# A decoder layer's MLP in exact fp32 parts: six pairs of first-product tiles by Strassen's algorithm, on one core

## The chip, the core and the metric

The kernel runs on one core of one Trainium2 chip. The metric is device time in microseconds (us) of one execution, the median of three runs. In the rows of the profile, PE is the matrix engine TensorE (PEld its weight loads), DVE is VectorE, ACT is ScalarE, POOL is GpSimd, and SP issues most of the loads. SBUF is the on-chip memory, PSUM the banks into which matmuls add (one bank holds 128 × 512 fp32 values).

## The reference

One layer of a hybrid decoder with 512 tokens and 1024 channels. The part in front of the MLP (token mixing by pooling and a state-space branch, gates, and an output product) gives h and is the same before and after. The change lies in the MLP:

```python
v = rmsnorm(h, mlp_norm_w[i])
hid = jax.nn.relu(v @ w_ff1[i])      # (512 x 1024) @ (1024 x 4096)
h = h + (hid * hid) @ w_ff2[i]       # (512 x 4096) @ (4096 x 1024)
out = rmsnorm(h, final_norm_w)
```

## The kernel before, in words

**Numbers.** Every fp32 value of a product is held as two parts of type fp32r: a high part, which ScalarE makes by a cast, and a low part, which VectorE makes by subtracting the high part from the value. A product of 128 × 128 weights with 512 columns then takes three matmuls: high × high, high × low, low × high. For a block of weights (128 × 1024) `split()` (L840 the cast to `shi`, L841 the subtraction to `slo`) or `block_part` (L75 `whi`, L76 `wlo`) does this. The pairs of parts come from a pool of four buffers, and a cast waits until the last matmul that reads the pair four splits before has ended.

**Chunks.** The MLP goes in eight chunks (`NC = 8`) of 512 hidden columns. In the first product a chunk has four tiles of 128 hidden columns by 512 tokens. `ff1_tile` computes one with 24 matmuls of 512 columns into one PSUM bank `pf` (L99 to L101), then ScalarE takes Relu (L1045) and Square (L1046) into the chunk's tile `r`, of which there is one buffer. PSUM for these tiles comes from a pool of four banks; from chunk 0's S1 on, that product's sums hold two of them, and the tiles have the other two. With the fourth tile the chunk's hidden values are split: `hh` (L1058) and `hl` (L1059) for the values themselves, then four sums of token and column halves into a tile of their own, `s` (L1061 to L1064), and their high and low parts (L1065, L1066), which read `s` and no longer `r`.

**Second product.** For chunks 0 to 6 it is done by Strassen's algorithm: seven products of 12 matmuls of 512 columns, A11, S2, S3, A22, S4, A12 and S1. Each takes one of seven parts of hh and hl (`prod`, L1079 to L1081) and one split block: a quarter of the second matrix (`b11`, `b12`, `b22`, `b21`) or a sum of quarters. The four sums of a chunk are made by `sum_of` on GpSimd (L1090): t1 = b11 + b12 in place, t2 = t1 + b22, b12 + b22, and t2 + b21. A11, S2, S3 and A22 add into the same two PSUM banks `alpha`; after each, VectorE adds the partial result to the output tile `ht` (`onto`, L906, 128 × 1024), and the next product's first matmul waits for that add. S4 starts `alpha` anew. A12 and S1 add up in banks of their own over chunks 0 to 6.

**Order.** The program is written in the order in which work is meant to run: after A11, S2, S3 and A22 stands one `filler()`, one tile of a later chunk's first product. The blocks of weights are loaded by the SP queue in the order of `_weight_blocks`. A scheduler then places the instructions of each engine; within an engine they run strictly in that order, each waiting for its inputs and its buffer. Six tiles of the first product run ahead of chunk 0's A11.

Of the kernel before, what the change touches and what calls it, by code (L numbers as in the profile page):

```python
# [51 lines left out]
def kernel(ctx: ExitStack, tc, xT, x, w, vec, fnw, out):  # L52
# [56 lines left out]
    dve.tensor_copy(ones_r, ones_f)
# [726 lines left out]
    def split(src):  # L836
        hi = wp.tile([P, 1024], F32R, tag="whi", name=f"shi{nsplit[0]}")
        lo = wp.tile([P, 1024], F32R, tag="wlo", name=f"slo{nsplit[0]}")
        nsplit[0] += 1
        act.copy(hi, src)  # L840
        dve.tensor_tensor(lo, src, hi.bitcast(F32), op=ALU.subtract)  # L841
# [190 lines left out]
    def ff1_tile(c, f):  # L1034
        if pf:
            ps = pf.pop(0)[0]
        else:
            p = ff1_begin(c, f)
            ff1_part(p, range(NK), True, True)
            ps = p[0]  # L1040
        if f == 0:
# [3 lines left out]
        act.activation(r, ps, AF.Relu)  # L1045
        act.activation(r, r, AF.Square)  # L1046
# [11 lines left out]
        act.copy(hh[:, :, :3, :], r[:, :, :3, :])  # L1058
        dve.tensor_tensor(hl[:, :, :3, :], r[:, :, :3, :], hh[:, :, :3, :].bitcast(F32), op=ALU.subtract)  # L1059
# [2 lines left out]
        dve.tensor_tensor(s[:, :, 1, :], s[:, :, 0, :], r[:, :, 2, :], op=ALU.subtract)
        dve.tensor_tensor(s[:, :, 2, :], r[:, :, 0, :], s[:, :, 1, :], op=ALU.add)
# [1 line left out]
        act.copy(hh[:, :, 3:, :], s)  # L1065
        dve.tensor_tensor(hl[:, :, 3:, :], s, hh[:, :, 3:, :].bitcast(F32), op=ALU.subtract)  # L1066
# [263 lines left out]
```

## Time and profile before

| what | value |
|---|---|
| median of three runs | 1008.87 us (1008.87 to 1009.21) |
| the profiled execution's time | 1009.23 us |
| its span | 1007.4 us |
| TensorE busy | 999.4 us, 99% |
| VectorE busy | 713.7 us, 71% |
| ScalarE busy | 556.4 us, 55% |
| GpSimd busy | 88.7 us, 9% |
| start of the first chunk's A11 | 704.32 us in the span |
| end of the last matmul | 1001.52 us |

A row of a timeline has the start, the duration, the engine, the line of the program, the operation, output and inputs, the shape; in brackets stands the idle time of the engine before the instruction and what ended it. A row of a group has the count and then busy time and the mean of one in ns. A row of stretches has the stretch, its length, and for each engine busy time and count.

### The profile page before, as it was taken

What the parts mean: (1) busy time and instruction counts of PE and PEld (TensorE: products, weight loads), DVE (VectorE), ACT (ScalarE), POOL (GpSimd) and SP (SyncE); (2) the same over time, 40 slices, a digit from 0 to 9 for tenths busy, and PEclk for the clock granted to TensorE, in tenths of its full rate; (3) what the DMA queues carried; (4) which work ended last, traced back from release to release, by engine and by line L of the source; (5) the groups of instructions that cost most, each with busy time, mean ns of one, the idle gap of its engine ahead of it and who ended that gap; (6) DMA issues with size and microseconds to landing.
All of it is one profiled execution on the core that took longest, in us unless ns stands there. A gap on an engine that the chain in (4) does not pass through costs nothing.

```text
span 1007.4 us, 14025 instructions
## 1 busy us (share of the span) xinstructions
PE 999.4 (99%) x5689; PEld 871.7 (87%) x5689; DVE 713.7 (71%) x896; ACT 556.4 (55%) x785; POOL 88.7 (9%) x52
## 2 busy tenths in 40 slices
PE   9999999999999999999999999999999999999997
PEld 8889999898889999888898888888888888888886
DVE  8978777776745588686765557985766677666866
ACT  7756859595843659574244333565545445354444
POOL 0000000000000000000000001003040430412400
PEclk9999999999999999999999999999999999999999
DMA  7243232323233232324433235042333324323112
GB/s 241 68 140 112 64 126 84 118 75 129 81 123 88 81 107 86 131 80 145 167 102 105 88 101 186 2 168 84 106 97 111 109 81 126 104 84 126 42 42 85
DMA packets 29283, 105.64 MB, mean 105 GB/s; under 512 B 3297, under 2 KB 4257, under 8 KB 28193
## 3 DMA queue, kind: packets, MB, share of 16 engines
q1 hardware_dynamic: 26496, 92.75, 28.8%
q0 software_dynamic: 2000, 11.08, 3.0%
q8 instruction: 45, 0.74, 0.3%
q10 hardware_dynamic: 720, 0.91, 0.2%
q14 instruction: 22, 0.17, 0.1%
HBM read 102.55 MB, written 2.16 MB: 104 GB/s over the span
## 4 chain that ended last, share of the span: by engine, by line
PE 96%; DVE 2%; DMA 1%; ACT 0%; SPq 0%; issue 0%; ACTq 0%
PE px L157 6%; PE pf L100 6%; PE pf L99 6%; PE pf L101 6%; PE px L158 6%; PE px L160 6%; PE alpha L1079 3%; PE alpha L1080 3%; PE alpha L1081 3%; PE pz L160 3%; PE pz L157 3%; PE pz L158 3%; PE pp L160 2%; PE pp L157 2%; PE pp L158 2%; PE py L509 2%
## 5 line engine op out<-in xcount | busy, mean ns | idle before, releaser
L76 DVE TENSOR_TENSOR wlo<-raw,whi 128x1024 fp32r<-128x1024 f32 (+1 forms) x131 | 163.9, 1252 | 114.9 <-ACT whi L75 114.6
L75 ACT CAST whi<-raw 128x1024 fp32r<-128x1024 f32 (+1 forms) x131 | 136.0, 1041 | 126.3 <-PE pf L100 55.8
L157 PE MATMUL px<-uh,whi 128*128 128x264 f32 (+1 forms) x448 | 118.9, 286 | 0.0
L158 PE MATMUL px<-ul,whi 128*128 128x264 f32 (+1 forms) x448 | 117.5, 283 | 0.0
L99 PE MATMUL pf<-vh,whi 128*128 128x512 f32 x256 | 99.8, 390 | 0.0
L101 PE MATMUL pf<-vh,wlo 128*128 128x512 f32 x256 | 99.6, 389 | 0.0
L100 PE MATMUL pf<-vl,whi 128*128 128x512 f32 x256 | 99.6, 389 | 0.0
L160 PE MATMUL px<-uh,wlo 128*128 128x264 f32 (+1 forms) x448 | 90.3, 283 | 0.0
L157 PEld LDWEIGHTS px<-uh,whi 128*128 128x128 f32 x448 | 84.8, 189 | 1.3 <-issue 1.0
L158 PEld LDWEIGHTS px<-ul,whi 128*128 128x128 f32 x448 | 84.4, 188 | 0.0
L841 DVE TENSOR_TENSOR slo<-b,shi 128x1024 fp32r<-128x1024 f32 x35 | 49.1, 1403 | 31.6 <-ACT shi L840 31.6
L160 PEld LDWEIGHTS px<-uh,wlo 128*128 128x128 f32 x448 | 68.8, 188 | 0.0
L840 ACT CAST shi<-b 128x1024 fp32r<-128x1024 f32 x35 | 36.8, 1050 | 47.2 <-PE pf L100 36.4
L99 PEld LDWEIGHTS pf<-vh,whi 128*128 128x128 f32 x256 | 48.1, 188 | 10.0
L101 PEld LDWEIGHTS pf<-vh,wlo 128*128 128x128 f32 x256 | 48.0, 188 | 10.0
L1090 POOL TENSOR_TENSOR b<-b,b 128x1024 f32<-128x1024 f32 x14 | 35.6, 2544 | 238.3 <-DVE slo L841 238.3
L100 PEld LDWEIGHTS pf<-vl,whi 128*128 128x128 f32 x256 | 48.1, 188 | 9.9
L1079 PE MATMUL alpha<-shi,hh 128*128 128x512 f32 x140 | 54.6, 390 | 0.0
L1081 PE MATMUL alpha<-shi,hl 128*128 128x512 f32 x140 | 54.5, 389 | 0.0
L1080 PE MATMUL alpha<-slo,hh 128*128 128x512 f32 x140 | 54.5, 389 | 0.0
L906 DVE TENSOR_TENSOR ht<-ht,alpha 128x1024 f32<-128x1024 f32 x35 | 42.5, 1215 | 10.9 <-PE alpha L1081 10.9
L157 PE MATMUL pz<-uh,whi 128*128 128x512 f32 x112 | 43.7, 390 | 0.0
(419 smaller groups left out, 2471.1 us busy)
## 6 DMA issues: line engine op xcount, KB each, us to landing
raw<-in_w SPq DMA_DIRECT2D x129, 512.0 KB, 3.6
b<-in_w SPq DMA_DIRECT2D x28, 512.0 KB, 3.5
abc<-acs_d POOLq DMA_DIRECT2D x8, 1024.0 KB, 5.2
wob<-in_w SPq DMA_DIRECT2D x8, 512.0 KB, 5.9
xt<-in_xT SPq DMA_DIRECT2D x8, 264.0 KB, 5.8
ht<-in_x POOLq DMA_DIRECT2D x4, 512.0 KB, 7.1
w<-in_w SPq DMA_DIRECT2D x4, 512.0 KB, 3.4
out_dram<-out SPq DMA_DIRECT2D x4, 320.0 KB, 2.4
```

The costliest lines, as they stand in the source:

```text
L75: act.copy(hi[:, c], raw[:, c])
L76: dve.tensor_tensor(lo[:, c], raw[:, c], hi[:, c].bitcast(F32), op=ALU.subtract)
L99: pe.matmul(ps, ah, bh, start=first, stop=False)
L100: pe.matmul(ps, ah, bl, start=False, stop=False)
L101: pe.matmul(ps, al, bh, start=False, stop=last)
L157: pe.matmul(o, wh, rhs[0][k][:, c], start=k == 0, stop=False)
L158: pe.matmul(o, wh, rhs[1][k][:, c], start=False, stop=False)
L160: pe.matmul(o, wl, rhs[0][k][:, c], start=False, stop=k == NK - 1)
L841: dve.tensor_tensor(lo, src, hi.bitcast(F32), op=ALU.subtract)
L1079: pe.matmul(ps[t], a[0], wh[:, cs], start=f, stop=False, skip_group_check=True)
L1080: pe.matmul(ps[t], a[0], wl[:, cs], start=False, stop=False, skip_group_check=True)
L1081: pe.matmul(ps[t], a[1], wh[:, cs], start=False, stop=l, skip_group_check=True)
```

## The change

In chunks 2 to 7 the tiles 2 and 3 of the first product (`PAIRS`) are no longer two plain tiles of 24 matmuls of 512 columns, but one generator `strassen(c, p)` with seven products of 12 matmuls of 256 columns. Their right-hand sides are halves of v and four sums of its halves, which `sum_halves` makes and splits on VectorE and ScalarE for four pairs of channel blocks: two pairs (k = 0, 1) along the first six tiles, one each within chunk 0 (k = 2, 3). Their weights are two raw blocks and three sums of their halves, made on VectorE. The products use two PSUM banks, `fb[0]` and `fb[1]`; partial results are copied out to `c01` and `r` and added up there by ScalarE and VectorE. All first-product tiles now use these two banks, the first ones too, which had four before.

To make room, the sums of the hidden halves are made in place in `r` (`hid_of`), so the tile `s` is gone, and four small tiles moved; the final norm's weights are loaded in chunk 6 instead of at the start of the MLP. The order of S4, S1, S2 and S3 among the seven segments is another one. The first product is no longer filled in by whole tiles: `fill()` and `step()` take half a plain tile or one product of a pair at a time, as many as a chunk's `due` asks for, after each product of the second matrix. `QUARTERS_AT` gives the load order to match. The sums of the second matrix stay on GpSimd. In the program after, `split` has lines L845 and L846, `block_part` L78 and L79, `onto` L909.

```diff
+QUARTERS_AT = (7, 12, 16, 20, 24, 28, 32, 32)
...
-    fw = hp_.tile([P, D], F32, name="fw")
...
-    nc.gpsimd.dma_start(fw, fnw.partition_broadcast(P))
...
+    VS = {}
+    sums = []
+    work = [hid.tile([P, 2, 7, 256], F32, tag=t, name=f"work_{t}").rearrange("p a s t -> p (a s t)")
+            for t in ("hh", "hl")]
+    part_of = lambda i: work[i // 3][:, 1024 * (i % 3) : 1024 * (i % 3) + 1024]
+    for k in range(4):
+        hs = [m1p.tile([P, SEQ], F32R, tag=f"m1_{d}", name=f"sh{d}") for d in (k, k + 4)]
+        lo = slp.tile([P, 4, 256], F32R, tag=f"sl{k}", name=f"sl{k}")
+        f = part_of(4 + k % 2)
+        f1, f2 = f[:, :512], f[:, 512:]
+        t = part_of(k).rearrange("p (s t) -> p s t", s=4)
+        sums.append((hs, lo, t, f1, f2, k))
+        VS["A11", k], VS["A12", k] = (vh[k][:, T1], vl[k][:, T1]), (vh[k + 4][:, T1], vl[k + 4][:, T1])
+        VS["A22", k] = vh[k + 4][:, T2], vl[k + 4][:, T2]
+        for n, name in enumerate(("S1", "S2", "S4", "S3")):
+            VS[name, k] = hs[n // 2][:, 256 * (n % 2) : 256 * (n % 2) + 256], lo[:, n, :]
+
+    def sum_halves(k):
+        hs, lo, t, f1, f2, k = sums[k]
+        dve.tensor_tensor(f1, vh[k].bitcast(F32), vl[k].bitcast(F32), op=ADD)
+        dve.tensor_tensor(f2, vh[k + 4].bitcast(F32), vl[k + 4].bitcast(F32), op=ADD)
+        dve.tensor_tensor(t[:, 0, :], f1[:, T2], f2[:, T2], op=SUB)
+        dve.tensor_tensor(t[:, 1, :], t[:, 0, :], f1[:, T1], op=SUB)
+        dve.tensor_tensor(t[:, 2, :], f2[:, T1], t[:, 1, :], op=ADD)
+        dve.tensor_tensor(t[:, 3, :], f1[:, T1], f1[:, T2], op=SUB)
+        fl2 = lambda a, n: a[:, 2 * n : 2 * n + 2, :].rearrange("p s t -> p (s t)")
+        for n in range(2):
+            act.copy(hs[n], fl2(t, n))
+            dve.tensor_tensor(fl2(lo, n), fl2(t, n), hs[n].bitcast(F32), op=SUB)
...
+    PAIRS = {(c, 1) for c in range(2, NC)}
+    fb = [p[0] for p in pf]
...
+    def hid_of(c):
         r = rel[c]
         hh = hid.tile([P, 2, 7, 256], F32R, tag="hh", name=f"hh{c}")
         hl = hid.tile([P, 2, 7, 256], F32R, tag="hl", name=f"hl{c}")
+        rel[c] = (hh, hl)
+        m = 4 if c == NC - 1 else 3
+        act.copy(hh[:, :, :m, :], r[:, :, :m, :])
+        dve.tensor_tensor(hl[:, :, :m, :], r[:, :, :m, :], hh[:, :, :m, :].bitcast(F32), op=ALU.subtract)
         if c == NC - 1:
-            act.copy(hh[:, :, :4, :], r)
-            dve.tensor_tensor(hl[:, :, :4, :], r, hh[:, :, :4, :].bitcast(F32), op=ALU.subtract)
-            rel[c] = (hh, hl)
             return
-
-        act.copy(hh[:, :, :3, :], r[:, :, :3, :])
-        dve.tensor_tensor(hl[:, :, :3, :], r[:, :, :3, :], hh[:, :, :3, :].bitcast(F32), op=ALU.subtract)
-        s = tmp.tile([P, 2, 4, 256], F32, tag="sums", name=f"s{c}")
-        dve.tensor_tensor(s[:, :, 0, :], r[:, :, 3, :], r[:, :, 1, :], op=ALU.subtract)
-        dve.tensor_tensor(s[:, :, 1, :], s[:, :, 0, :], r[:, :, 2, :], op=ALU.subtract)
-        dve.tensor_tensor(s[:, :, 2, :], r[:, :, 0, :], s[:, :, 1, :], op=ALU.add)
-        dve.tensor_tensor(s[:, :, 3, :], r[:, :, 2, :], r[:, :, 3, :], op=ALU.subtract)
-        act.copy(hh[:, :, 3:, :], s)
-        dve.tensor_tensor(hl[:, :, 3:, :], s, hh[:, :, 3:, :].bitcast(F32), op=ALU.subtract)
-        rel[c] = (hh, hl)
+        dve.tensor_tensor(r[:, :, 1, :], r[:, :, 3, :], r[:, :, 1, :], op=ALU.subtract)
+        dve.tensor_tensor(r[:, :, 3, :], r[:, :, 2, :], r[:, :, 3, :], op=ALU.subtract)
+        dve.tensor_tensor(r[:, :, 2, :], r[:, :, 1, :], r[:, :, 2, :], op=ALU.subtract)
+        dve.tensor_tensor(r[:, :, 0, :], r[:, :, 0, :], r[:, :, 2, :], op=ALU.add)
+        act.copy(hh[:, :, 3:, :], r)
+        dve.tensor_tensor(hl[:, :, 3:, :], r, hh[:, :, 3:, :].bitcast(F32), op=ALU.subtract)
...
+    def strassen(c, p):
+        raw = []
+        for i in range(2):
+            b = nblk[0]
+            nblk[0] += 1
+            t = wp.tile([P, 1024], F32, tag="raw", name=f"raw{b}", bufs=3)
+            nc.sync.dma_start(t, w[b])
+            raw.append(t)
+        C1, C2 = slice(0, 512), slice(512, 1024)
+        t12 = wp.tile([P, 1024], F32, tag="raw", name=f"t12_{c}_{p}", bufs=3)
+        dve.tensor_tensor(t12[:, C2], raw[0][:, C1], raw[1][:, C1], op=ADD)
+        dve.tensor_tensor(t12[:, C1], t12[:, C2], raw[1][:, C2], op=ADD)
+        dve.tensor_tensor(raw[1][:, C1], raw[1][:, C1], raw[1][:, C2], op=ADD)
+        wA = split(raw[0])
+        yield 0
+        one, two = bank(), bank()
+        nth[0] += 1
+        al, be_, ga, de = one[:, T1], two[:, T2], two[:, T1], two[:, T2]
...
+        r = rel_of(c)[:, p]
+        product(al, "A11", wA, 0, True, False)
+        act.copy(c01[:, 0, :], al)
+        wB = split(t12)
+        yield 1
+        product(be_, "A12", wA, 512, True, True)
+        dve.tensor_tensor(c01[:, 0, :], c01[:, 0, :], be_, op=ADD)
+        dve.tensor_tensor(t12[:, C1], t12[:, C1], raw[0][:, C2], op=ADD)
+        yield 1
+        product(al, "S2", wB, 0, False, False)
+        act.copy(c01[:, 1, :], al)
+        wC = split(raw[1])
+        yield 1
+        product(ga, "S1", wB, 512, True, True)
+        dve.tensor_tensor(c01[:, 1, :], ga, c01[:, 1, :], op=SUB)
+        act.copy(r[:, 3, :], ga)
+        yield 1
+        product(al, "S3", wC, 0, False, False)
+        dve.tensor_tensor(r[:, 3, :], r[:, 3, :], al, op=SUB)
+        wD = split(t12[:, C1])
+        yield 1
+        product(de, "S4", wC, 512, True, True)
+        dve.tensor_tensor(c01[:, 1, :], c01[:, 1, :], de, op=ADD)
+        yield 1
+        product(al, "A22", wD, 0, False, True)
+        act.activation(r[:, 0:3:2, :], c01, AF.Relu)
+        act.activation(r[:, 1, :], al, AF.Relu)
+        act.activation(r[:, 3, :], r[:, 3, :], AF.Relu)
+        rf = r.rearrange("p s t -> p (s t)")
+        act.activation(rf, rf, AF.Square)
+        if p == 1:
+            hid_of(c)
+        yield 1
...
+    for n in range(6):
+        step()
+        step()
+        if n in (4, 5):
+            sum_halves(n - 4)
...
-    def filler():
-        if order:
-            ff1_tile(*order.pop(0))
+    due = [0, 0]
+
+    def fill(n=1):
+        due[0] += n * due[1]
+        while due[0] > 0.5 and (items or live):
+            due[0] -= step()

     for c in range(NC - 1):
+        assert nblk[0] - ff0 - 4 * c == QUARTERS_AT[c], (c, nblk[0] - ff0 - 4 * c)
         b11, b12, b22, b21 = (quarter(n) for n in ("b11_", "b12_", "b22_", "b21_"))
         z, e = c == 0, c == NC - 2
+        if c < NC - 3:
+            rest = sum(i[4] for i in items if i[1] < c + 2 or (i[1] == c + 2 and (i[2] == 0 if i[0] is strassen else i[2] < 2)))
+        else:
+            rest = sum(i[4] for i in items)
+        rest += sum(l[1] if l[1] > 2 else 2 * l[1] for l in live)
+        due[1] = rest / (7 if c < NC - 3 else 10 if c == NC - 3 else 3)
         prod(av, c, A11, split(b11), True, False)
         onto(0, 0, alpha, ADD)
         t1 = sum_of(b11, b12, "", b11)
         t2 = sum_of(t1, b22, f"t2_{c}")
-        filler()
+        fill()
         prod(av, c, S2, split(t2), False, False)
         onto(0, 1, alpha, SUB)
-        filler()
+        fill()
+        if z:
+            sum_halves(2)
         prod(av, c, S3, split(sum_of(b12, b22, "", b12)), False, False)
         onto(1, 1, alpha, SUB)
-        filler()
+        fill()
         prod(av, c, A22, split(sum_of(t2, b21, "", t2)), False, True)
         onto(1, 0, alpha, ADD)
+        if z:
+            sum_halves(3)
+        if e:
+            while items or live:
+                step()
+        else:
+            fill()
+        w22 = split(b22)
         if e:
             prod(q5v, c, S1, split(t1), z, True)
             for t in range(2):
                 onto(0, 1, q5v[t], ADD, t)
                 onto(1, 1, q5v[t], ADD, t)
-        elif c < NC - 3:
-            filler()
-        prod(av, c, S4, split(b22), True, True)
+            fw = slp.tile([P, D], F32, tag="sl1", name="fw")
+            nc.gpsimd.dma_start(fw, fnw.partition_broadcast(P))
+            junk2.append(m1p.tile([P, SEQ], F32, tag="m1_3", name="junk2"))
+        prod(av, c, S4, w22, True, True)
         onto(0, 1, alpha, ADD)
+        if not e:
+            fill()
         prod(p2v, c, A12, split(b21), z, False)
         if not e:
+            fill()
             prod(q5v, c, S1, split(t1), z, False)
-    assert not order
+            fill()
+    assert not items and not live
```

VectorE round A11 of chunk 0, before. `s` is the tile of hidden sums, `hl` the low parts of the hidden values, `slo` and `wlo` low parts of weights; L906 is the add of A11.

```order
L841 TENSOR_TENSOR slo_6673<-b_113_6664,shi_6672 128x1024
L76 TENSOR_TENSOR wlo_6694<-raw_6692,whi_6693 128x1024
L1061 TENSOR_TENSOR s_6582<-r_6507 128x2x256
L1064 TENSOR_TENSOR s_6582<-r_6507 128x2x256
L1062 TENSOR_TENSOR s_6582<-s_6582,r_6507 128x2x256
L1059 TENSOR_TENSOR hl_6579<-r_6507,hh_6578 128x2x768
L1063 TENSOR_TENSOR s_6582<-r_6507,s_6582 128x2x256
L841 TENSOR_TENSOR slo_6726<-t_0_6690,shi_6725 128x1024
L1066 TENSOR_TENSOR hl_6579<-s_6582,hh_6578 128x2x1024
L76 TENSOR_TENSOR wlo_6744<-raw_6742,whi_6743 128x1024
L906 TENSOR_TENSOR ht<-ht,alpha 128x2x512
```

VectorE at the same place, after. `r` is the hidden tile, now with the sums in it; L1048 to L1057 belong to `sum_halves`; L909 is the add of A11.

```order
L1052 TENSOR_TENSOR work_hh<-work_hl,work_hh 128x256
L1053 TENSOR_TENSOR work_hh<-work_hl 128x256
L1057 TENSOR_TENSOR sl_6513<-work_hh,sh_6511 128x512
L1048 TENSOR_TENSOR work_hl<-vh_6091,vl_6099 128x512
L1049 TENSOR_TENSOR work_hl<-vh_6095,vl_6103 128x512
L1096 TENSOR_TENSOR hl_6603<-r_6527,hh_6602 128x2x1024
L1057 TENSOR_TENSOR sl_6513<-work_hh,sh_6512 128x512
L1050 TENSOR_TENSOR work_hh<-work_hl 128x256
L1053 TENSOR_TENSOR work_hh<-work_hl 128x256
L1051 TENSOR_TENSOR work_hh<-work_hh,work_hl 128x256
L909 TENSOR_TENSOR ht<-ht,alpha 128x2x512
L1052 TENSOR_TENSOR work_hh<-work_hl,work_hh 128x256
```

The sums of v's halves stand between the hidden tile's sums (L1091 to L1094) and their low parts (L1096), and again between those and the add of A11. The split for S2 (`slo<-t`) now stands behind that add.

ScalarE at this place, before: `r` of chunk 1 is written (L1045) after the cast of chunk 0's sums from `s` (L1065).

```order
L1045 ACTIVATE r_6507<-pf_3_6551 128x512
L1046 ACTIVATE r_6507<-r_6507 128x512
L1058 CAST hh_6578<-r_6507 128x2x768
L840 CAST shi_6725<-t_0_6690 128x1024
L1065 CAST hh_6578<-s_6582 128x2x1024
L1045 ACTIVATE r_6620<-pf_0_6595 128x512
L1046 ACTIVATE r_6620<-r_6620 128x512
L75 CAST whi_6743<-raw_6742 128x1024
```

ScalarE, after. The Relu (L1111) of chunk 1's first two tiles writes into `r`, whose buffer the operation L1096 on VectorE reads last.

```order
L1087 CAST hh_6602<-r_6527 128x2x768
L78 CAST whi_6734<-raw_6733 128x1024
L1056 CAST sh_6511<-work_hh 128x512
L1095 CAST hh_6602<-r_6527 128x2x1024
L1056 CAST sh_6512<-work_hh 128x512
L845 CAST shi_6751<-t_0_6731 128x1024
L78 CAST whi_6783<-raw_6782 128x1024
L1111 ACTIVATE r_6642<-pf_0_6415 128x512
L1111 ACTIVATE r_6642<-pf_1_6448 128x512
L1112 ACTIVATE r_6642<-r_6642 128x512 x2
```

The two Relus stand behind the casts of the split for S2 and of the next block, and are next to each other.

VectorE from the split of chunk 1's b11 (`slo<-b_121`) to its add of A11 and on to S2's, before:

```order
L841 TENSOR_TENSOR slo_6947<-b_121_6938,shi_6946 128x1024
L906 TENSOR_TENSOR ht<-ht,alpha 128x2x512
L76 TENSOR_TENSOR wlo_6968<-raw_6966,whi_6967 128x1024
L841 TENSOR_TENSOR slo_7000<-t_1_6964,shi_6999 128x1024
L76 TENSOR_TENSOR wlo_7018<-raw_7016,whi_7017 128x1024
L906 TENSOR_TENSOR ht<-ht,alpha 128x2x512
```

VectorE from the split of chunk 1's b11 (`slo<-b_123`) to its add of A11, after. `t_2_1` is the tile `t12` of chunk 2's pair, `t_1` is t2 of chunk 1.

```order
L846 TENSOR_TENSOR slo_7009<-b_123_7000,shi_7008 128x1024
L1096 TENSOR_TENSOR hl_6843<-r_6642,hh_6842 128x2x1024
L846 TENSOR_TENSOR slo_7042<-t_2_1_6950,shi_7041 128x1024
L1157 TENSOR_TENSOR t_2_1_6950<-t_2_1_6950,raw_6946 128x512
L846 TENSOR_TENSOR slo_7060<-t_1_7026,shi_7059 128x1024
L909 TENSOR_TENSOR ht<-ht,alpha 128x2x512
```

Before, the add of A11 stands next behind the split of b11, and the split of t2 two places after the add; after, four operations stand between b11's split and the add of A11, and the split of t2 is one of them.

More of the change, by code (lines that the diff above doesn't have):

```diff
@@ new lines, with prime, step @@
+    items = []
+    for c in range(NC):
+        for p in range(2):
+            items += [(strassen, c, p, 7, 7)] if (c, p) in PAIRS else [(plain, c, 2 * p + i, 2, 4) for i in range(2)]
+    live = []
+    def prime(n):
+        while len(live) < n and items:
+            fn, c, x, steps, cost = items.pop(0)
+            g = fn(c, x)
+            next(g)
+            live.append([g, steps])
+    def step():
+        prime(1)
+        g = live[0]
+        g[1] -= 1
+        if g[1] <= 1:
+            prime(2)
+        cost = next(g[0])
+        if not g[1]:
+            live.pop(0)
+        return cost
@@ L1185 @@
                 if t not in outs:
[L1186 removed]
+                    o = (tmp, "relu") if t == 0 else (slp, f"sl{(0, 0, 2, 3)[t]}")
+                    outs[t] = o[0].tile([P, D], F32, tag=o[1], name=f"out{t}")
                 dve.tensor_tensor(outs[t][:, cs], ht[:, t, cs], fw[:, cs], op=ALU.mult)
```

97 lines of the change are left out of this document (61 added, 36 removed).

## The prediction

> **What bounds the kernel now.** I read the page first, then the busy time by stretches of one chunk, then TensorE's instructions in order of time for the pitch of a matmul, and last the timelines of VectorE, GpSimd and ScalarE round a chunk's start.
>
> ```profile
> span 1007.4 us, 14025 instructions
> PE 999.4 (99%) x5689; PEld 871.7 (87%) x5689; DVE 713.7 (71%) x896; ACT 556.4 (55%) x785; POOL 88.7 (9%) x52
> ...
> PE 96%; DVE 2%; DMA 1%; ACT 0%; SPq 0%; issue 0%; ACTq 0%
> ```
>
> ```profile
> 671.00:712.00 41.00, 41.00 (x185) 33.95 (x184) 27.67 (x29) 20.65 (x29) 10.54 (x4) 1.00 0.33 116
> 756.00:797.00 41.00, 41.00 (x182) 33.97 (x181) 27.74 (x22) 19.19 (x21) 11.35 (x4) 1.00 0.34 103
> ```
>
> The columns of the stretches are length, then busy time of PE, PEld, DVE, ACT and POOL, granted clock, DMA share, GB/s. TensorE has no idle time in the MLP; VectorE is busy 27.7 of 41 us, GpSimd 11. So a shorter list of matmuls shows in the time at once, if nobody makes TensorE wait.
>
> ```profile
> 739.68 0.39 PE L1079 MATMUL p<-shi,hh 128*128 128x512 f32 x1
> ...
> 744.89 0.39 PE L1081 MATMUL q<-shi,hl 128*128 128x512 f32 x1
> ...
> 998.49 0.28 PE L1180 MATMUL pl<-shi,hh 128*128 128x256 f32 x1
> ...
> 1001.24 0.28 PE L1180 MATMUL last<-shi,hl 128*128 128x256 f32 x1
> ```
>
> Both stretches run back to back and hold 23 steps each: (744.89 − 739.68)/23 = 0.2265 us for 512 columns, (1001.24 − 998.49)/23 = 0.1196 us for 256.
>
> **Matmuls removed and added.** A pair of tiles took 2 × 8 × 3 = 48 matmuls of 512 columns; by Strassen it takes 7 × 4 × 3 = 84 of 256. Six pairs: 288 × 0.2265 = 65.2 us go, 504 × 0.1196 = 60.3 us come. **TensorE's work: −5.0 us.** Two matmuls of 256 columns take 0.239 us against 0.2265 for one of 512, so the eighth of the work that Strassen saves shrinks to 7.7%. The Trainium skill, "TensorE: Matmul & The Clock Gate", Part 2, gives a gap of N/2.4 + 2.5 ns; by it the six pairs would save an estimated 7.1 us. The measured pitches decide.
>
> **What shares VectorE's time.** The quarter sums of the second matrix stay on GpSimd, four in a chunk, and VectorE gets more to do in the same chunk. How the two go together is in these rows:
>
> ```profile
> 780.12 2.41 POOL L1090 TENSOR_TENSOR b<-b,b 128x1024 f32<-128x1024 f32 x1 [28.21 <-DVE slo L841]
> 782.61 3.25 POOL L1090 TENSOR_TENSOR t<-b,b 128x1024 f32<-128x1024 f32 x1
> 785.82 2.40 POOL L1090 TENSOR_TENSOR b<-b,b 128x1024 f32<-128x1024 f32 x1
> ...
> 941.45 2.40 POOL L1090 TENSOR_TENSOR t<-b,b 128x1024 f32<-128x1024 f32 x1
> 943.81 3.38 POOL L1090 TENSOR_TENSOR b<-b,b 128x1024 f32<-128x1024 f32 x1
> ```
>
> ```profile
> 778.81 1.23 DVE L841 TENSOR_TENSOR slo<-b,shi 128x1024 fp32r<-128x1024 f32 x1 [3.12 <-ACT shi L840]
> 780.68 1.22 DVE L906 TENSOR_TENSOR ht<-ht,alpha 128x1024 f32<-128x1024 f32 x1 [0.64 <-PE alpha L1081]
> 781.82 1.79 DVE L76 TENSOR_TENSOR wlo<-raw,whi 128x1024 fp32r<-128x1024 f32 x1
> 786.98 2.32 DVE L841 TENSOR_TENSOR slo<-t,shi 128x1024 fp32r<-128x1024 f32 x1 [3.37 <-ACT shi L840]
> ...
> 942.02 2.91 DVE L76 TENSOR_TENSOR wlo<-raw,whi 128x1024 fp32r<-128x1024 f32 x1
> 944.97 3.31 DVE L841 TENSOR_TENSOR slo<-t,shi 128x1024 fp32r<-128x1024 f32 x1
> ```
>
> A VectorE operation with both inputs in SBUF and a GpSimd sum never run together. The one at 942.02 ends at 944.93, 1.08 us after the sum that ends at 943.85; the next sum, issued at 943.81, takes 3.38 because it waits for that; the next VectorE operation ends 1.09 us after it. They alternate, 2.40 us for a sum. The add from PSUM at 780.68 isn't touched. In this kernel VectorE has gaps, and the sums fall into them. Pitches of VectorE alone, and a cast:
>
> ```profile
> 764.87 0.68 DVE L1062 TENSOR_TENSOR s<-s,r 128x512 f32<-128x512 f32 x1
> 765.47 1.75 DVE L1059 TENSOR_TENSOR hl<-r,hh 128x1536 fp32r<-128x1536 f32 x1
> 767.14 0.68 DVE L1063 TENSOR_TENSOR s<-r,s 128x512 f32<-128x512 f32 x1
> ...
> 770.01 2.28 DVE L1066 TENSOR_TENSOR hl<-s,hh 128x2048 fp32r<-128x2048 f32 x1
> 772.21 1.22 DVE L841 TENSOR_TENSOR slo<-b,shi 128x1024 fp32r<-128x1024 f32 x1
> 773.35 1.21 DVE L906 TENSOR_TENSOR ht<-ht,alpha 128x1024 f32<-128x1024 f32 x1
> ...
> L840 ACT CAST shi<-b 128x1024 fp32r<-128x1024 f32 x35 | 36.8, 1050 | 47.2 <-PE pf L100 36.4
> ...
> L816 DVE TENSOR_TENSOR m<-m,acc 128x256 f32<-128x256 f32 x4 | 1.7, 418 | 0.0
> ```
>
> From start to start: 0.60 for 512 columns, 1.67 for 1536, 2.20 for 2048, 1.14 for 1024; 256 columns 0.34 (0.418 less the same 0.08 of overlap).
>
> **VectorE's load in a chunk.** Now: seven splits and five adds of 1024, two plain splits, 3.5 splits of Strassen blocks, four sums of block halves, four of PSUM quarters, and the hidden tile's 1.67 + 2.20 + 4 × 0.60. That is (7 + 5 + 2 + 3.5) × 1.14 + 4 × 0.60 + 4 × 0.34 + 6.27 = 30 us, and 4 × 2.40 of GpSimd beside it, of which only the 7 us of PSUM reads can overlap: 32 to 40 us against a chunk of 41 − 0.9 = 40. It may just fit on average; what counts is the order.
>
> **Chunks 1 to 5, the second product.**
>
> ```profile
> 785.92 0.39 PE L1079 MATMUL alpha<-shi,hh 128*128 128x512 f32 x1
> 788.64 0.39 PE L99 MATMUL pf<-vh,whi 128*128 128x512 f32 x1
> 794.08 0.39 PE L1079 MATMUL alpha<-shi,hh 128*128 128x512 f32 x1
> ```
>
> S2 adds into the banks of A11, so it must wait for VectorE's add of A11. It now starts 8.16 us after A11; a 5.44 us tile lies between. After the change A11 (2.72) and two Strassen products (24 × 0.1196 = 2.87) give 5.59. Call A11's start 0. The cast of b11 waits for a split buffer that product A12 frees, three half products (8.16 us) ahead; with 1.05 for the cast and 1.22 for the subtraction the split ends at −5.7 (now at 780.04, 5.9 ahead). Then GpSimd starts three sums, and VectorE has, in this order, the 2048 part of hl, the split of t12, a half sum of t12, the split of t2, and only then the add of A11. The port's line: 3 × 2.40 + 2.20 + 1.14 + 0.60 + 1.14 = 12.3, to +6.6; the add 1.2, to 7.8. S2 starts 2.3 us late. Later steps have 1.4 us or more to spare (S3 and A22, with GpSimd done) or over 3 us (copies of the PSUM quarters), so I take nothing there. Ends: 1.3, if one operation slips in free, and 3.3, if one sum more is met. **Five chunks: +11.5 us (6.5 to 16.5).**
>
> **Chunk 0.**
>
> ```profile
> 693.41 1.06 ACT L75 CAST whi<-raw 128x1024 fp32r<-128x1024 f32 x1 [3.23 <-PE pf L100]
> 694.37 0.58 ACT L1045 ACTIVATE r<-pf 128x512 f32<-128x512 f32 x1
> 694.99 0.63 ACT L1046 ACTIVATE r<-r 128x512 f32<-128x512 f32 x1
> 695.65 1.48 ACT L1058 CAST hh<-r 128x1536 fp32r<-128x1536 f32 x1
> ...
> 702.63 1.92 ACT L1065 CAST hh<-s 128x2048 fp32r<-128x2048 f32 x1 [2.69 <-DVE s L1063]
> ```
>
> ```profile
> 704.32 0.39 PE L1079 MATMUL alpha<-shi,hh 128*128 128x512 f32 x1
> ...
> 707.04 0.39 PE L99 MATMUL pf<-vh,whi 128*128 128x512 f32 x1
> ```
>
> The sums are now made in place in r, which has one buffer, and only two PSUM banks take first products. So the Relu of chunk 1 waits for the last reader of chunk 0's r, the 2048 part of hl, and the tile due at 707.04 waits for that Relu. Between stand the new sum_halves. With ScalarE's rows as they are, b11's cast ends at 694.5 and its split at 695.7; GpSimd's first sum to 698.15; hl (1.67) to 699.8; a sum to 702.2; one 512 sum to 702.8; the third sum to 705.2. Then eight operations of 512, four of 256 and the 2048: 8 × 0.60 + 4 × 0.34 + 2.20 = 8.4, to 713.6; Relu 0.6, 714.2. **TensorE stands 7.2 us.** After that VectorE still has two of the four sum_halves between the splits of S2, S3 and A22: by the same count S3's add comes 1.35 late, its split 1.05, others 0.6, if TensorE runs at full speed.
>
> ```profile
> 1.51 3.91 PE L201 MATMUL pdt<-ones_r 128*128 128x512 f32 x9 [1.51 <-DVE ones_r L109]
> ...
> 1004.00:1007.40 3.40, 0.00 (x0) 0.00 (x0) 0.00 (x0) 0.00 (x0) 0.00 (x0) 0.65 0.40 154
> ```
>
> It won't: the mean clock of 0.65 in the last stretch means half clock from 1005.0 on, 3.5 us after the last matmul's end at 1001.52, and the first nine matmuls of the program took 0.43 us each. A 7 us pause would cost some eight matmuls 0.2 us more, 1.6 us, and in that time VectorE catches up. So 7.2 and about 3 for both together. **Chunk 0: +10 us (5 to 13).**
>
> **Chunk 6** has three Strassen products before S2 (7.03 us after A11), but hl stands before b11's split, which ends at −2.0, and one split more (raw) stands before the add: −2.0 + 7.2 + 2.9 + 1.2 = 9.3, and t2's split 1.14 later; its low half is due at 7.26. **+3 us (1.5 to 4).**
>
> The rest: the same count of weight loads in another order at a DMA share of 0.33, and fnw's load, last in GpSimd's queue; taken at nothing, hidden behind TensorE's 40 us a chunk (ends 0 and +2). The tail has the same operations, and the first product sequences up to 671 are the same.
>
> **Sum:** −5.0 + 10 + 11.5 + 3 = +19.5. The profiled execution took 1009.23 us (its span 1007.4 and 1.8 round it), the median of the runs 1008.87, so I give 1028.5. The likeliest case's own range adds the ends above: 1017 to 1038.
>
> **Rivals.**
> 1. *VectorE is hidden; not slower.* One mechanism: the new sums and splits don't exclude GpSimd's, because their place in the queue leaves the port to GpSimd while VectorE waits for ScalarE. In chunks 1 to 5 t2 is then ready in time, the add of A11 runs at 2.9 to 4.1, before 5.59; in chunk 0 the line is 7.2 − 5.6 = 1.6 us late. −5.0 + 1.6: about 1005.5. It decides at 12.3 us of port work against 11.3 us between b11's split and S2's start, less the add. For it: all four sums of a chunk are hidden now. Against it: every overlap in the rows above is paid in full. The Trainium skill, "SBUF — State Buffer", section on who interferes with whom, calls the shared port pair an exclusive lock held for the whole instruction; by that rule, with which 2.91 and 3.31 us agree, this rival falls.
> 2. *Only chunk 0 waits.* In chunks 1 to 5 the split buffer for b11 comes free one half product (2.7 us) earlier than I read, and the burst is over before A11's add. −5.0 + 10: 1014.
> 3. *The lateness spreads.* With VectorE 2.3 us late, the PSUM quarters of Strassen, which have 3 to 3.5 us, are missed as well once a load or cast is another 1 us late: two more waits of about 1.5 us in each of six chunks, +18: 1046.
>
> **Chances.** Forecast 0.62, rival 2 0.13, rival 1 0.13, rival 3 0.12. Range 1008 to 1046: it takes in rival 2 down to chunk 0's lower end (−5.0 + 5, 1009) and rival 3 up to its middle, and leaves out rival 1 and the other half of rival 3, 0.19. A measurement tells about 0.2% (2 us) from no change: faster 0.12 (rival 1, mostly), within 0.02, slower 0.86.
>
> **What would show it.** Right: 256-column matmuls at 0.12 us; in chunk 0 a pause of some 7 us before the tile that follows A11, with VectorE busy throughout and a dip of granted clock; in chunks 1 to 5 one idle piece of about 2.3 us ahead of S2, released by VectorE's add, with VectorE operations of 2 to 3.5 us beside GpSimd's sums. Wrong: TensorE still at 99% in the MLP's stretches, or pauses elsewhere (before a Strassen product, by a ScalarE copy).

## The result, and the profile after

The changed kernel takes 1025.43 us (1025.23 to 1027.56), the kernel before 1009.04 us beside it: ratio 1.0168 (95% interval 1.0155 to 1.018). Forecast were 1028.5 us, 1008 to 1046, slower with 0.86.

The page of the kernel after (span, busy times, and the shares of the chain that ended last):

```profile
span 1023.7 us, 14586 instructions
PE 999.0 (98%) x5905; PEld 880.3 (86%) x5905; DVE 781.6 (76%) x988; ACT 575.6 (56%) x823; POOL 97.6 (10%) x52
...
PE 79%; DVE 11%; ACT 4%; issue 4%; DMA 1%; POOL 1%; SPq 0%; POOLq 0%; ACTq 0%
```

TensorE's share of the chain falls from 96% to 79%: now it waits for others. Whom, the waits of TensorE tell (total, times, longest):

```profile
PE alpha L1218 <- DVE ht L909: 8.6, 5, 1.7
PE pf L102 <- ACT r L1111: 6.7, 1, 6.7
...
PE pf L1146 <- ACT r L1111: 0.8, 1, 0.8
PE alpha L1219 <- DVE slo L846: 0.6, 1, 0.6
```

The five waits of 1.7 us are S2's first matmul in chunks 1 to 5, behind VectorE's add of A11; the 6.7 is the tile behind A11 of chunk 0. The page counts a matmul as busy to its modelled end, so the time lost is a little more: start to start less the pitch, it is 1.9 where the page has 1.7.

Chunk 2, timelines of VectorE, of GpSimd and of TensorE:

```profile
789.75 1.23 DVE L846 TENSOR_TENSOR slo<-b,shi 128x1024 fp32r<-128x1024 f32 x1 [0.39 <-ACT shi L845]
791.56 4.03 DVE L1096 TENSOR_TENSOR hl<-r,hh 128x2048 fp32r<-128x2048 f32 x1 [0.59 <-ACT hh L1095]
797.20 1.75 DVE L846 TENSOR_TENSOR slo<-t,shi 128x1024 fp32r<-128x1024 f32 x1 [1.60 <-ACT shi L845]
798.98 2.78 DVE L1157 TENSOR_TENSOR t<-t,raw 128x512 f32<-128x512 f32 x1
801.68 1.21 DVE L846 TENSOR_TENSOR slo<-t,shi 128x1024 fp32r<-128x1024 f32 x1
802.82 1.21 DVE L909 TENSOR_TENSOR ht<-ht,alpha 128x1024 f32<-128x1024 f32 x1
```

```profile
791.05 2.39 POOL L1229 TENSOR_TENSOR b<-b,b 128x1024 f32<-128x1024 f32 x1 [27.76 <-DVE slo L846]
793.53 4.34 POOL L1229 TENSOR_TENSOR t<-b,b 128x1024 f32<-128x1024 f32 x1
797.83 3.39 POOL L1229 TENSOR_TENSOR b<-b,b 128x1024 f32<-128x1024 f32 x1
```

```profile
804.08 0.50 PE L1218 MATMUL alpha<-shi,hh 128*128 128x512 f32 x1 [1.71 <-DVE ht L909]
```

The half sum of 512 columns, 0.68 us for that size in the rows of the prediction, takes 2.78: it waits for the third sum, which ends at 801.22. Split and add follow, the add ends at 804.03, and S2 starts 0.05 later.

### The profile page after: what moved, and what is told of

The parts are those of the page before. It is cut to its first block, busy times and chain, and to the rows that moved or that the text cites. A ratio compares the mean times of both kernels' runs of the same rounds, so it can differ in the third digit from the quotient of the medians.

```text
span 1023.7 us, 14586 instructions
## 1 busy us (share of the span) xinstructions
PE 999.0 (98%) x5905; PEld 880.3 (86%) x5905; DVE 781.6 (76%) x988; ACT 575.6 (56%) x823; POOL 97.6 (10%) x52
## 4 chain that ended last, share of the span: by engine, by line
PE 79%; DVE 11%; ACT 4%; issue 4%; DMA 1%; POOL 1%; SPq 0%; POOLq 0%; ACTq 0%
PE px L160 6%; PE px L161 6%; PE px L163 6%; PE pz L163 3%; DVE slo L846 3%; PE pz L160 3%; PE pz L161 3%; PE alpha L1218 2%; PE alpha L1219 2%; PE alpha L1220 2%; DVE hl L1096 2%; ACT shi L845 2%; PE pp L160 1%; PE pp L163 1%; PE pp L161 1%
## 5 line engine op out<-in xcount | busy, mean ns | idle before, releaser
L79 DVE TENSOR_TENSOR wlo<-raw,whi 128x1024 fp32r<-128x1024 f32 (+1 forms) x119 | 144.1, 1213 | 91.4 <-ACT whi L78 91.1
L78 ACT CAST whi<-raw 128x1024 fp32r<-128x1024 f32 (+1 forms) x119 | 123.3, 1039 | 86.1 <-issue 21.4
L102 PE MATMUL pf<-vh,whi 128*128 128x512 f32 x160 | 63.3, 396 | 6.7 <-ACT r L1111 6.7
L1229 POOL TENSOR_TENSOR b<-b,b 128x1024 f32<-128x1024 f32 x14 | 40.9, 2918 | 241.2 <-DVE slo L846 185.7
L103 PE MATMUL pf<-vl,whi 128*128 128x512 f32 x160 | 62.8, 393 | 0.0
L104 PE MATMUL pf<-vh,wlo 128*128 128x512 f32 x160 | 62.8, 392 | 0.0
L845 ACT CAST shi<-b 128x1024 fp32r<-128x1024 f32 x35 | 36.8, 1052 | 41.1 <-PE pf L103 17.3
L846 DVE TENSOR_TENSOR slo<-b,shi 128x1024 fp32r<-128x1024 f32 x35 | 42.5, 1220 | 5.9 <-ACT shi L845 5.8
L909 DVE TENSOR_TENSOR ht<-ht,alpha 128x1024 f32<-128x1024 f32 x35 | 42.5, 1213 | 5.8 <-PE alpha L1220 5.8
L845 ACT CAST shi<-t 128x1024 fp32r<-128x1024 f32 (+1 forms) x26 | 24.7, 950 | 38.3 <-PE alpha L1220 27.7
L163 PE MATMUL pz<-uh,wlo 128*128 128x512 f32 x112 | 43.6, 390 | 0.0
L161 PE MATMUL pz<-ul,whi 128*128 128x512 f32 x112 | 43.6, 389 | 0.0
```

The source lines that it names most:

```text
L78: act.copy(hi[:, c], raw[:, c])
L79: dve.tensor_tensor(lo[:, c], raw[:, c], hi[:, c].bitcast(F32), op=ALU.subtract)
L102: pe.matmul(ps, ah, bh, start=first, stop=False)
L103: pe.matmul(ps, ah, bl, start=False, stop=False)
L161: pe.matmul(o, wh, rhs[1][k][:, c], start=False, stop=False)
L163: pe.matmul(o, wl, rhs[0][k][:, c], start=False, stop=k == NK - 1)
```

## The experiments

Each kernel is the changed one with the edit shown, unless another is named. Time lost in TensorE's rows is counted as above (start to start, less the pitch of the matmul), over all places where it is more than 0.05 us, from 690 us on: 20.8 us in the changed kernel, 0.2 before. Where a pause and the slower clock behind it are told apart, the first is the pause itself and the second what the matmuls behind it take beyond their pitch.

**e1, sums on VectorE.**

```diff
-        pool.tensor_tensor(t, a, b, op=ADD)
+        dve.tensor_tensor(t, a, b, op=ADD)
```

> The second matrix's four sums of a chunk on VectorE instead of GpSimd, nothing else. Theory (VectorE's two-input SBUF operations and GpSimd's sums take turns, 2.4 us for a sum): a sum costs VectorE 1.14 us in place of 2.40 us of waiting, so the burst between b11's split and the add of A11 gets 3.8 us shorter; the add in chunks 1 to 5 is done before S2 is due and its 2.0 us of waiting goes (about -11 with what follows it), chunk 6's 1.3 too. In chunk 0 some 5 of 8.5 us stay, since the halves' sums are still there. 1011 us (1007 to 1014), no VectorE operation above 1.3 us for 1024 columns in the MLP. Rival (VectorE simply has too much work): 4 x 1.14 us more in each chunk, slower than 1025, up to 1050. Rival (the order or the buffer alone makes the waits, GpSimd's sums beside it cost nothing): 1025 to 1040.

Measured: 1008.37 us, ratio to before 0.9998 (0.9989 to 1.0007). TensorE's waits of e1 in the MLP, and two groups of VectorE (the splits for S2, S3 and so on; the hidden sums' low parts):

```profile
PE pf L102 <- ACT r L1111: 2.4, 1, 2.4
...
PE alpha L1218 <- DVE ht L909: 0.3, 1, 0.3
```

```profile
L846 DVE TENSOR_TENSOR slo<-t,shi 128x1024 fp32r<-128x1024 f32 x20 | 24.4, 1219 | 0.0
L1096 DVE TENSOR_TENSOR hl<-r,hh 128x2048 fp32r<-128x2048 f32 x7 | 16.0, 2284 | 0.8 <-ACT hh L1095 0.8
```

The same groups of the changed kernel:

```profile
L1096 DVE TENSOR_TENSOR hl<-r,hh 128x2048 fp32r<-128x2048 f32 x7 | 23.0, 3287 | 3.2 <-ACT hh L1095 3.2
L846 DVE TENSOR_TENSOR slo<-t,shi 128x1024 fp32r<-128x1024 f32 x20 | 29.5, 1477 | 9.9 <-ACT shi L845 9.9
```

28 more operations on VectorE make the kernel 17 us faster. Too much work on VectorE isn't the cause, nor is the order alone. 5.3 us are still lost, 4.2 of them in chunk 0.

**e2, the halves' sums early.**

```diff
-        if n in (4, 5):
-            sum_halves(n - 4)
+        if n < 4:
+            sum_halves(n)
...
-        if z:
-            sum_halves(2)
...
-        if z:
-            sum_halves(3)
```

> The four sums of v's halves run along the first four tiles (VectorE has 11 idle us there) instead of round A11 of chunk 0. Theory A (chunk 0's pause is a chain: b11's split, three sums on GpSimd in turn with VectorE, then the in-place sums 2.4, cast 1.9, low parts 2.2, Relu 0.6): the pause before the tile behind A11 shrinks only from 6.8 to 5.8 us, clock loss stays: 1024 (1022 to 1025). Theory B (the operations of sum_halves that stand between are the cause, as the prediction counts them, 4.4 us): pause 2.4 us without a loss of clock, 1019.

Measured: 1025.59 us, above the range of theory A (1022 to 1025) and far from theory B. Theory B falls: with no operation of `sum_halves` in between, the pause is not 2.4 but 7.9 us. Theory A has the kind but not the size (5.8 us). VectorE, e2, in chunk 0:

```profile
699.45 3.23 DVE L79 TENSOR_TENSOR wlo<-raw,whi 128x1024 fp32r<-128x1024 f32 x1
702.60 2.88 DVE L1091 TENSOR_TENSOR r<-r 128x512 f32<-128x512 f32 x1
705.51 2.75 DVE L1092 TENSOR_TENSOR r<-r 128x512 f32<-128x512 f32 x1
708.29 0.69 DVE L1093 TENSOR_TENSOR r<-r 128x512 f32<-128x512 f32 x1
709.01 0.69 DVE L1094 TENSOR_TENSOR r<-r 128x512 f32<-128x512 f32 x1
711.67 2.29 DVE L1096 TENSOR_TENSOR hl<-r,hh 128x2048 fp32r<-128x2048 f32 x1 [1.96 <-ACT hh L1095]
```

Each sum on GpSimd lets one VectorE operation past, long or short. So the in-place sums wait for the third one in any case, and then come the cast and the subtraction that free r. The early halves also move four scalings of `ht` to this place, and the split of b11 ends at 697.67, 2.0 us later than in the changed kernel, while A11 runs 0.4 us earlier (its last matmul starts at 706.32 in place of 706.76). Without these 2.4 us the pause would be an estimated 5.5 us in place of 6.7, near theory A's 5.8; so `sum_halves` was worth about 1.2 us of it.

**e3, chunk 0's sums in tiles apart.**

```diff
+        if c == 0:
+            for p in range(2):
+                s = slp.tile([P, 4, 256], F32, tag=f"sl{2 + p}", name=f"s0_{p}")
...
+                act.copy(hh[:, p, 3:, :], s)
```

> Chunk 0's hidden sums go into tiles of their own (the ones that later hold the low parts of v's last two pairs of halves), so r comes free with the last sum; all other chunks as in the changed kernel. Theory A (VectorE's burst itself is too long): the pause before the tile behind A11 goes, but the add of A11 and the split for S2 still end at 716 to 718, and S2, due at 709.7, waits some 7 us instead: 1025 (1022 to 1026). Theory B (the single buffer of r is the cause): 1017 to 1018.

Measured: 1023.84 us; the pause in front of the tile is gone and stands at the next deadline. Waits of e3:

```profile
PE alpha L1230 <- DVE ht L909: 13.9, 6, 5.7
```

S2 of chunk 0 starts at 715.99, 5.7 idle us late. Chunk 0 loses 8.3 us in all, 8.4 in the changed kernel: the buffer decides where TensorE waits, and hardly how long.

**e4, no Strassen pairs** (and no sums of halves; the load order is set to match).

```diff
-    PAIRS = {(c, 1) for c in range(2, NC)}
+    PAIRS = set()
```

> No Strassen pairs and no sums of v's halves: all 32 first-product tiles plain, the rest (in-place sums, half tiles after each product, two banks, new places of tiles) as in the changed kernel. Theory: chunks 1 to 5 have no wait, since neither the split of t12 nor the half sum stands between b11's split and the add, and the hidden low parts come ahead; chunk 0 still waits 5 to 6 us plus 1.6 of clock by the in-place chain beside GpSimd's sums: 1016 (1012 to 1018). Rival (the pairs alone make all the loss): 1009. Rival (the finer filling or the in-place sums make the waits of chunks 1 to 5): 1025 to 1031.

Measured: 1023.49 us, outside the range of the theory (1012 to 1018) and of both rivals. My theory falls here: chunks 1 to 5 wait too.

```profile
PE pf L102 <- ACT r L1111: 5.6, 1, 5.6
PE alpha L1218 <- DVE ht L909: 4.0, 6, 1.1
```

14.2 us are lost with no pair in the kernel, 6.6 fewer than with the pairs, but the pairs' saving of TensorE's work is gone as well. Chunk 0 loses 5.8 us by the pause and 2.8 by the slower clock behind it, each of chunks 1 to 5 loses 0.8, and chunk 6 loses 1.4. Of S2's 2.0 us in chunks 1 to 5 the pairs' operations make 1.2 at most. The rest comes with the other edits: S2 is due 5.44 us after A11, and the split of a block and the split of t2 stand ahead of the add.

**e5, one sum of four on VectorE** (b12 + b22).

```diff
-        prod(av, c, S3, split(sum_of(b12, b22, "", b12)), False, False)
+        prod(av, c, S3, split(sum_of(b12, b22, "third", b12)), False, False)
...
+        (dve if name == "third" else pool).tensor_tensor(t, a, b, op=ADD)
```

> As the changed kernel, but one of the four sums of a chunk, b12 + b22, the third that GpSimd starts behind b11's split, is made on VectorE, where it stands between the low parts of the hidden sums and the split of t12. A dose between the changed kernel (S2 waits 2.0 us in each of chunks 1 to 5) and e1 (0 to 0.5). Theory (turns): the burst loses 2.40 of waiting and gains 1.14, so S2 waits 0.7 to 0.9 us in chunks 1 to 5, 6 us less in all with chunk 6; chunk 0's pause shrinks by about 1: 1018.5 (1016 to 1021). Rival (more work on VectorE is what hurts): 1.1 us more in each chunk, 1030. Rival (any sum left on GpSimd keeps the whole wait, since t2 is what S2 waits for): 1024 to 1026.

Measured: 1019.81 us. Waits of e5:

```profile
PE pf L102 <- ACT r L1111: 5.8, 1, 5.8
PE alpha L1218 <- DVE ht L909: 3.8, 5, 0.8
```

S2 waits 0.8 in place of 1.7 us. A turn of 2.40 exchanged for an operation of 1.14 would give 1.26; 0.96 was found. S2 doesn't need this sum. It needs t2, which is still GpSimd's and comes no sooner (797.92 in chunk 2, 797.87 in the changed kernel). So the rival that GpSimd hurts only by handing over t2 late falls too.

**e6 and e7, chunk 0 cleared.** In e6 the halves' sums run early, along the first three tiles, and chunk 0's hidden sums go into the scratch tile of the halves' sums; e7 is e6 with the edit of e1.

```diff
+        if c == 0:
+            s = work[0][:, :2048].rearrange("p (a s t) -> p a s t", a=2, s=4)
```

> The sums of v's halves along the first four tiles, and chunk 0's hidden sums in a tile apart (the scratch of the halves' sums), so neither the single r nor sum_halves stands in chunk 0's way; GpSimd keeps its four sums. Theory (turns with GpSimd are enough by themselves): b11's split ends near 702, three sums at 2.4 us alternate with 2.2, 1.14 and 1.14 on VectorE, the add of A11 ends near 714.8, and S2, due at 709.7, waits some 5 us and loses 1.6 to the clock: 1023.5 (1021 to 1025). Rival (chunk 0's pause is the sum of halves and r's buffer): no pause in chunk 0, 1017.

> e6 with the second matrix's sums on VectorE: Strassen pairs, no buffer wait in chunk 0, no sums on GpSimd. Theory: the add of A11 ends near 708.8 in chunk 0, S2 waits in no chunk by more than 0.5 us, and what is left is TensorE's saving of 5.0 us (4.9 by the pitches of the runs so far): 1004.5 (1003.5 to 1006), faster than before by 0.4%. Rival (VectorE at 90% of the time loses it again somewhere): 1008 to 1012.

Measured: e6 1022.39 us; e7 1004.39 us, ratio to before 0.9953 (0.994 to 0.9966). Waits of e6:

```profile
PE alpha L1227 <- DVE ht L909: 12.9, 6, 5.1
```

The page of e7, a stretch of one chunk in it (length; busy PE, PEld, DVE, ACT, POOL; clock), and its last matmul:

```profile
span 1002.9 us, 14585 instructions
PE 995.0 (99%) x5905; PEld 878.4 (88%) x5905; DVE 774.0 (77%) x1016; ACT 577.2 (58%) x823; POOL 9.9 (1%) x24
```

```profile
756.00:797.00 41.00, 41.00 (x223) 35.65 (x222) 36.09 (x37) 22.61 (x27) 0.00 (x0) 1.00 0.36 105
```

```profile
996.63 0.28 PE L1353 MATMUL last<-shi,hl 128*128 128x256 f32 x1
```

VectorE is busy 36 of 41 us and TensorE never waits in the MLP. Against 1001.24 before, the last matmul starts 4.6 us sooner: TensorE's saving, alone. e6 differs from e7 in the engine of the sums only, and loses 18 us.

**e8, the control:** the kernel before with the edit of e1.

> The kernel before with its four sums of a chunk on VectorE instead of GpSimd: the control. Theory: VectorE has gaps there and TensorE never waits for it with the sums on GpSimd, so nothing changes in the time: 1008.9 (within 1), while VectorE's operations of 1024 columns all take 1.2 us. Rival (the sums beside it cost the kernel before something too): 1 to 4 us faster. Rival (VectorE's work alone): slower by 2 us or more.

Measured: 1009.29 us, ratio 1.0003 (0.9993 to 1.0012): there the engine of the sums makes no difference.

**e9, a double share behind A11.**

```diff
-        fill()
+        fill(1 if e else 2)
         prod(av, c, S2, split(t2), False, False)
...
             prod(q5v, c, S1, split(t1), z, False)
-            fill()
+            if c == NC - 3:
+                fill()
```

> The changed kernel with the same work and GpSimd's sums, but a double share of the first product behind A11 and none behind S1 (chunks 0 to 4; chunk 5 only the double share), so S2 is due some 8.4 us after A11 instead of 5.6 (8.16 in the kernel before). Theory (the burst of 12 to 13 us is late by 2 us only because S2 is due 2.6 us sooner than before): S2's wait in chunks 1 to 5 and most of chunk 6's goes, chunk 0's pause in front of the tile stays with its clock: 1015 (1013 to 1018). Rival (VectorE has too much work in a chunk, so the wait comes back at a later product or split): 1020 to 1026.

Measured: 1042.5 us, far outside the ranges of the theory and of the rival. S2's wait in chunks 1 to 5 is gone, as said, but the forecast time is missed: the wait comes back, larger, inside the pair, and chunk 6, where it was to shrink, waits 3.5 us. Waits of e9, VectorE in chunk 2, and TensorE in chunks 1 and 2:

```profile
PE pf L1146 <- DVE c L1156: 13.6, 5, 3.4
...
PE alpha L1218 <- DVE ht L909: 3.5, 1, 3.5
```

```profile
802.50 3.42 DVE L846 TENSOR_TENSOR slo<-raw,shi 128x1024 fp32r<-128x1024 f32 x1
805.84 1.21 DVE L909 TENSOR_TENSOR ht<-ht,alpha 128x1024 f32<-128x1024 f32 x1
806.97 1.21 DVE L846 TENSOR_TENSOR slo<-t,shi 128x1024 fp32r<-128x1024 f32 x1
808.11 0.41 DVE L1156 TENSOR_TENSOR c<-c,pf 128x256 f32<-128x256 f32 x1
```

```profile
765.72 0.39 PE L1146 MATMUL pf<-sh,shi 128*128 128x256 f32 x1 [3.44 <-DVE c L1156]
...
808.57 0.58 PE L1146 MATMUL pf<-sh,shi 128*128 128x256 f32 x1 [2.53 <-DVE c L1156]
```

With the pair's products close together, its product S1 needs the bank that the pair's A12 left, and the add that reads this bank (L1156) stands behind the same burst. The share taken from behind S1 also brings b11's split nearer to A11, 2.7 us ahead of it in chunk 2 (796.19) in place of 5.7, so the burst starts 3 us later. Four pauses of 2.5 us also cost the clock: the matmuls behind each come at 0.21 us in place of 0.12. Of 36.5 us lost, 21 go to these places in chunks 1 to 5, 9.7 to chunk 0 and 5.5 to chunk 6; what makes chunk 6 worse is not shown.

**e10, the kernel before with half tiles** (chunks 0 to 4; one behind each product, two behind S2).

```diff
-        filler()
+        h = c < NC - 3
+        filler(1 if h else 2)
         prod(av, c, S2, split(t2), False, False)
```

> The kernel before, unchanged but for the filling of chunks 0 to 4: the four tiles are split into eight half tiles, one behind each of the seven products and two behind S2, so S2 is due 5.44 us after A11 instead of 8.16. No Strassen pairs, no in-place sums, four sums on GpSimd. Theory (the sums on GpSimd were hidden before only because S2 had 8.16 us): b11's split, three sums of 2.40 in turn with three splits of 1.14, then the add of 1.14 end 5.9 to 7 us after A11's start; S2 waits 0.5 to 1.5 us in chunks 1 to 4 and 1 to 3 in chunk 0: 1014 (1011 to 1017). Rival (the finer filling is harmless, and only the in-place sums and the pairs' operations make the waits): 1009 within 1.5.

Measured: 1011.69 us, ratio 1.0027 (1.0016 to 1.0038): inside the theory's range, near its lower end, and not by the way that it named. S2 waits 0.9 us in chunk 0 and nowhere else:

```profile
PE alpha L1085 <- DVE ht L906: 0.9, 1, 0.9
```

2.6 us are lost in all, the others mostly in pieces of 0.3 before S4. So the shorter way from A11 to S2 is nearly harmless by itself; in chunk 2 of this kernel b11's split ends 7.6 us ahead of A11, in e4 only 4.5, and in the changed kernel 5.7. What makes the wait is the nearer deadline together with the later split: with the early split and the near deadline (e10) chunks 1 to 4 don't wait, and with a late split and the far deadline (e9) the add of A11 ends 8.2 us behind A11's start in chunk 2, in time for an S2 that is due after 8.4.

## Why the prediction was right

| step | forecast | found |
|---|---|---|
| TensorE's work | −5.0 | −4.6 (e7, in which nothing waits) |
| chunk 0 | +10: 7.2, and 3 for clock and late halves | +8.4: 6.8, and 1.5 of clock |
| chunks 1 to 5, S2 | +11.5: 2.3 each | +9.9: 2.0 each |
| a place not foreseen, chunk 1 | 0 | +1.0 |
| chunk 6 | +3 | +1.3 |
| sum | +19.5 | +16.0; the spans differ by 16.3 |

The kind and the main places came as forecast. That the sum came within 3.5 us is in a small part luck: three terms were too large by 1.6 to 1.7 us each, and a saving 0.4 smaller and a place of 1.0 that was not foreseen took back 1.4.

**Pitches.** 60.3 us for the 504 new matmuls hold: they run at 0.12 us, and e7 is faster than before by 4.7 us (1009.11 − 1004.39). The Trainium skill's gap ("TensorE: Matmul & The Clock Gate", Part 2) would have made this an estimated 7.1 us; the runs show 4.6.

**Turns.** The step that carries the forecast is that a sum on GpSimd and an operation of VectorE with two SBUF inputs exclude each other. e1, e5 and e6 against e7 show it, with the sums' engine as the one difference, and e8 shows that it costs nothing where there is room. Rival 1 falls. The Trainium skill, "SBUF — State Buffer", section on who interferes with whom, says the same of the shared port pair; here it is 3.29 us in place of 2.28 for the mean of the 2048-column subtraction.

**Chunks 1 to 5.** In chunk 2, b11's split ends at 790.98, 5.7 us ahead of A11, as counted, and the add ends 7.4 us behind A11's start where the count gave 7.8. What the account left out is that S2 would wait 0.8 us without the pairs' operations too (e4): only some 1.2 of the 2.0 us are theirs. Two of its sums are a little off: from 7.8 and 5.59 S2 is 2.2 us late, not 2.3, and the upper ends of the likeliest case add up to 1039, not 1038. Nothing hangs on either.

**Chunk 0.** The pause came at the place named, 6.8 for 7.2 us, and as an account of VectorE's queue the count holds: the third sum ends at 704.84 (705.2 in the count), the low parts at 713.15 (713.6), with VectorE busy in all 20 us from 700 to 720, and the granted clock at 0.83 (length; busy PE, PEld, DVE, ACT, POOL; clock, DMA share, GB/s):

```profile
700.00:720.00 20.00, 13.32 (x53) 10.59 (x52) 20.00 (x25) 8.16 (x11) 5.01 (x3) 0.83 0.07 20
```

What the count has wrong is the worth of one term. It has 3.8 us of `sum_halves` in this line (4 × 0.60 + 4 × 0.34), and e2 shows that without them the pause is only some 1.2 us shorter. For behind the in-place sums stands a cast of 1.9 us (708.50 to 710.40), which the count has nowhere; with `sum_halves` VectorE works through it, without them it waits for it. So the chain is: three sums in turn with whatever VectorE has next, then the in-place sums, the cast, the low parts and the Relu:

```profile
707.79 0.68 DVE L1094 TENSOR_TENSOR r<-r 128x512 f32<-128x512 f32 x1
...
710.87 2.28 DVE L1096 TENSOR_TENSOR hl<-r,hh 128x2048 fp32r<-128x2048 f32 x1
```

```profile
713.83 0.79 PE L102 MATMUL pf<-vh,whi 128*128 128x512 f32 x1 [6.68 <-ACT r L1111]
714.42 0.63 PE L103 MATMUL pf<-vl,whi 128*128 128x512 f32 x1
```

The 3 us for a slow clock and late halves were 1.5, all clock: seven matmuls at 0.38 to 0.59 us, five of them at 0.43, where the forecast had eight and 1.6 us; no later step of chunk 0 waits.

**Chunk 6** was mis-sized: 3 forecast, 1.3 found (0.25 before S2's first matmul, 0.9 before its second, 0.1 behind it). **Chunk 1** has 1.0 us at a place that I took at nothing: in ScalarE's queue the Relu (757.96) stands behind the cast of t2, which waits 3.79 us for GpSimd's sum:

```profile
757.01 1.05 ACT L845 CAST shi<-t 128x1024 fp32r<-128x1024 f32 x1 [3.79 <-POOL t L1229]
757.96 0.59 ACT L1111 ACTIVATE r<-pf 128x512 f32<-128x512 f32 x1
```

Rival 2 (only chunk 0 waits) and rival 3 (the lateness spreads) did not come about here; e9 shows that rival 3's mechanism exists one step of order away.

What stays open is how far the in-place sums alone bring b11's split 3 us nearer to A11 in e4 than in e10; no run changes them alone in chunks 1 to 5. The traces point at them. In chunk 2 the hidden tile's first cast starts 19.6 us ahead of A11 in e4 and 19.8 in e10, so little of it comes before that cast, where the two PSUM banks would act. But in e10 the sums begin with that cast, while in e4 the first in-place sum starts 4.7 us behind it (780.97), since it overwrites what the first part of the low parts (L1088) still reads. The second cast, behind which the cast of b11 stands on ScalarE, starts 11.0 us ahead of A11 in e4 and 15.6 in e10. These are its rows, e4 and then e10:

```profile
784.87 1.92 ACT L1095 CAST hh<-r 128x2048 fp32r<-128x2048 f32 x1 [1.35 <-DVE r L1094]
```

```profile
771.90 1.91 ACT L1071 CAST hh<-s 128x2048 fp32r<-128x2048 f32 x1 [1.76 <-DVE s L1069]
```

Two buffers of r in every chunk weren't tried.

## What to carry to other kernels

An engine that seems free can be paid for by another one: before moving work beside GpSimd's two-input sums, count each sum as time taken from VectorE, and ask by when the product behind it is due. A saving on the bounding engine is kept only if the feeders keep their slack; here the change cost 16 us with the sums on GpSimd, about nothing with the sums on VectorE, where a sum costs 1.14 us in place of 2.40 (e1), and was worth −4.6 us once chunk 0 was cleared as well (e7). Removing one late wait shows the next: judge by the sum of waits, not by the one that the profile names first.

## What the runs showed of the hardware

The drop of TensorE's clock goes by no fixed length of a pause. The five pauses of 1.7 us in the changed kernel left it at full speed; in e1 one of 2.35 us was enough, in e9 four of 2.53 us, and one of 3.44 us in e9 was not (the matmuls behind 765.72 come at 0.12 us). In e1 TensorE was running again when it slowed:

```profile
709.19 0.50 PE L102 MATMUL pf<-vh,whi 128*128 128x512 f32 x1 [2.35 <-ACT r L1111]
...
710.36 0.63 PE L103 MATMUL pf<-vl,whi 128*128 128x512 f32 x1
```

The Trainium skill, "TensorE: Matmul & The Clock Gate", Part 1, names an idle window of about 3.4 us, free-running; that the window runs free agrees with this scatter, but 2.35 us of idle time were enough here.
